# Quarter products with the weights' leading parts of both halves first, and three pieces moved in a two-layer encoder's feed-forward blocks

## The chip, the core and the metric

The kernel runs on one core of one Trainium2 chip. The metric is the device time of one execution in microseconds (us), lower is better. The core has four engines that matter here, each with a queue of its own that it works through in order: TensorE (PE in the profile, with PEld for its loads of the stationary operand), VectorE (DVE), ScalarE (ACT) and GpSimd (POOL). SP only issues DMA transfers.

## The reference

Two encoder layers over 512 tokens of width 1024. Each layer has a feed-forward block, an attention mixer, cross-attention to a memory, and a second feed-forward block. The change lies in the four feed-forward blocks, each of which computes

```
h = h + 0.5 * swiglu(rmsnorm(h, g), wg, wu, wd)

def swiglu(x, wg, wu, wd):
    return (jax.nn.silu(x @ wg) * (x @ wu)) @ wd        # 1024 -> 2816 -> 1024
```

in float32. In the order of the program they are called here the first to the fourth feed-forward block (layer 0 ffn1, ffn2, layer 1 ffn1, ffn2).

## The kernel before

A float32 operand is split in two parts: a leading part, rounded by ACT (`wh`, `sh`, `xh`, `t1h`, ...), and the rest, subtracted by DVE (`wl`, `sl`, `xl`, `t1l`, ...). A product of two split operands is three matmuls: leading by leading, leading weights by lower tokens, lower weights by leading tokens, the pairs (0, 0), (0, 1), (1, 0) in the code.

The 2816 hidden columns are 22 blocks of 128, taken in 11 pairs. Pair 0, the plain pair, is computed directly (`plain_pair`, into four banks of PSUM: a gate bank and an up bank for each of its two blocks). Its end, `plain_end`, turns the norm's factors into a tile R (four transposes and a DVE copy, L421), multiplies the two gate banks by R (the plain gate, L424) and calls `hidden`: Silu on ACT (L432) and two multiplications with the up banks on DVE (L434).

The ten other pairs use a scheme with seven products instead of eight over quarters: the 1024 rows are two halves of 4 tiles, the 512 tokens two halves of 256, and gate and up are the two column halves. A quarter of the weights is a 128x1024 tile (2 blocks z by 4 row tiles k); a token operand is one of x's quarters (`xs`) or one of the sums t1 to t4. `product` issues the matmuls of one quarter product: 2 z by 3 pairs of parts by 4 k, 24 matmuls of 128x256 into a bank whose left half holds z = 0 and whose right half z = 1. Per pair they are named by their token operand:

- `open_pair`: "11" into bank y, then a copy of y: for pair 1 into a corner of the result tile `gu` (L592), for later pairs into a second bank x (L595).
- `sum_pair`: "1" into bank z, "2" added onto y; then ACT copies y to `gu` (L619).
- `cross_pair`: "21" into x (for pair 1 a fresh bank, added to the copy by L630), "3" onto y; copies and sums follow (L644 on ACT, L645 on DVE).
- `close_pair`: "4" onto y (`lower`), "22" onto z (`upper`); it returns `gates`, which runs a pair later.

Before a product may add onto a bank, the copy or sum that reads the bank must be done. The leading part of a quarter that needs a sum (`s`, L611 and L661 on DVE) is made by ACT at L544, its lower part by DVE at L546. `wh` and `wl` have two buffers each, `sh` and `sl` one, so a new `wh` waits until PE has read an old one for the last time. The tile `gu` shares two buffers with the tiles `tq` that hold t1 to t4 before they are split.

The down products (h @ wd) come in three chunks. The first two are quarter products too (`paired_down`), the last (pairs 7 to 10) is direct: `down_products`, L844, 128x512 matmuls with weights `sh`, `sl` for the first output block. Some of that block's products are put around the last pair's closing, to keep PE supplied.

The code is written stage by stage. A scheduler then fixes the order of each engine's queue and the buffers; `high_priority()` lets what is in it go ahead of other work, and `behind(ins)` keeps what is in it after the instruction ins. So a line that moves in the code can move others in the queues.

Of the kernel before, what the change touches and what calls it, by code (L numbers as in the profile page):

```python
# [11 lines left out]
F32 = mybir.dt.float32  # L12
# [7 lines left out]
P = 128  # L20
S = 512
# [91 lines left out]
class Encoder:  # L113
# [205 lines left out]
    def ffn(self, pre):  # L319


        with ExitStack() as ctx:
            pool = lambda name: ctx.enter_context(self.tc.tile_pool(name=pre + name, bufs=1))
            f = self.f = SimpleNamespace(pre=pre, ctx=ctx, hp=pool("h"), tp=pool("t"), H={}, n=2, taken=None, own=False, low=None, gate=None, ahead=None, spread=None, macc=None,
                                        G=[])
            R = self.plain_pair()
            ends = [sum(CHUNKS[:c + 1]) // 2 for c in range(len(CHUNKS))]
            c = 0
            pair = self.open_pair(1)
            R()  # L330
            for p in range(1, FB // 2):
                final = p == FB // 2 - 1
                self.sum_pair(pair)
                hide = None
                if f.gate is not None:
                    f.gate, gate = None, f.gate
                    hide = gate(f.lowered)
                if p in ends and c not in PAIRED:
                    self.down(c)
                    c += 1  # L340
                self.cross_pair(pair)
                if hide is not None:
                    hide()
                if p == 2:
                    self.set_aside()
                if final:
                    early = self.block(c, 0, True)
                    f.ahead = self.leading
                    self.down_products(c, early, LEAD + REST, False, range(CHUNKS[c] - 4))
                    self.down_products(c, early, LEAD + REST, False, range(CHUNKS[c] - 4, CHUNKS[c] - 2))  # L350
                    self.close_pair(pair, True)
                    self.down(c, early)
                else:
                    old, pair = pair, self.open_pair(p + 1)
                    f.gate = self.close_pair(old, False)
                    if c in PAIRED and p == ends[c]:
                        if self.mem_r is None and c == 0:
                            self.mem_squares()
                        self.paired_down(c)
                        c += 1  # L360
                if self.mem_r is None:
                    self.mem_stats(p)
# [51 lines left out]
    def plain_end(self, banks, r):  # L414
        nc, f = self.nc, self.f
        p = self.bank("pb")
        f.R = f.tp.tile([P, S], F32, name="R", tag="R", bufs=1)
        with self.tc.high_priority():
            for i in range(QB):
                nc.tensor.transpose(p[:, i * P:(i + 1) * P], r[:, i:i + 1].to_broadcast([P, P]), self.ident)  # L420
            nc.vector.tensor_copy(f.R, p)  # L421
        gs = f.tp.tile([P, 1024], F32, name="gs", tag="gs")
        for b in range(2):
            f.gated = nc.vector.tensor_mul(gs[:, b * S:(b + 1) * S], banks[b][0], f.R)  # L424
        self.hidden(0, gs, [pp[1] for pp in banks])

    def hidden(self, p, gs, us):

# [132 lines left out]
    def product(self, bank, w, xs, first, late=False):  # L561

        half = len(xs)
        ops = [(z, a, b, k) for z in range(2) for a, b in ((0, 0), (0, 1), (1, 0)) for k in range(half)]
        if late:
            ops.sort(key=lambda op: op[3] == half - 1)
        for n, (z, a, b, k) in enumerate(ops):
            o = (z * half + k) * P
            self.nc.tensor.matmul(bank[:, z * 256:z * 256 + 256], w[a][:, o:o + P], xs[k][b],  # L569
                                  start=first and n == 0, stop=n == len(ops) - 1, skip_group_check=True)  # L570
# [8 lines left out]
    def open_pair(self, p):  # L579
        nc, f = self.nc, self.f  # L580
        pair = SimpleNamespace(p=p)
        pair.y = self.bank("pa")
        with self.tc.high_priority():
            pair.w11 = self.raw_quarter(p, 0)
            f.first = f.after
            if f.spread is not None and p == 1:
                f.after = self.loaded
            w = self.operand(pair.w11)
        self.product(pair.y, w, self.tokens("11"), True)
        pair.gu = f.tp.tile([P, 2048], F32, name="gu", tag="gu", bufs=2)  # L590
        if p == 1:
            nc.scalar.copy(self.corner(pair, 0, 0), self.halves(pair.y))  # L592
        else:
            pair.x = self.bank("pa")
            nc.scalar.copy(pair.x, pair.y)  # L595
        return pair

    def sum_pair(self, pair):

        nc, f, p = self.nc, self.f, pair.p  # L600
        pair.z = self.bank("pb")
        with self.tc.high_priority():
            pair.s = f.tp.tile([P, 1024], F32, name="s1", tag="s1", bufs=3)
            self.fetch(pair.s, p, 3, f.first)
            nc.gpsimd.dma_start(pair.s, self.quarter(p, 2), accum_op=OP.add)
            w = self.operand(pair.s, None, f.factored if p == 1 else None)
        with self.tc.high_priority():
            xs = self.tokens("1")
        self.product(pair.z, w, xs, True)
        with self.tc.high_priority():  # L610
            f.lowered = nc.vector.tensor_sub(pair.s, pair.s, pair.w11)  # L611
            if p == 2:
                f.low(f.lowered)
            xs = self.tokens("2")
            w = self.operand(pair.s)
            f.lowered = self.parted
        self.product(pair.y, w, xs, False)
        with self.tc.high_priority():
            nc.scalar.copy(self.corner(pair, 0, 1), self.halves(pair.y))  # L619

    def cross_pair(self, pair):
        nc, f, p = self.nc, self.f, pair.p
        with self.tc.high_priority(), self.behind(f.lowered if p == 1 else None):
            pair.w12 = self.raw_quarter(p, 1)
            w = self.operand(pair.w12)
        x = self.bank("pa") if p == 1 else pair.x
        self.product(x, w, self.tokens("21"), p == 1)
        c = self.corner(pair, 0, 0)
        if p == 1:
            nc.vector.tensor_add(c, c, self.halves(x))  # L630
        else:
            nc.scalar.copy(c, self.halves(x))
        with self.tc.high_priority():
            s = f.tp.tile([P, 1024], F32, name="s3", tag="s3", bufs=1)
            self.fetch(s, p, 2)
            with self.behind(f.led), self.behind(f.taken):
                nc.scalar.activation(s, s, AF.Copy, scale=-1.0)  # L637
            nc.gpsimd.dma_start(s, self.quarter(p, 0), accum_op=OP.add)  # L638
            w = self.operand(s)
            f.crossed = self.parted  # L640
        self.product(pair.y, w, self.tokens("3"), False)
        c = self.corner(pair, 1, 1)
        with self.tc.high_priority():
            f.taken = nc.scalar.copy(c, self.halves(pair.y))  # L644
        nc.vector.tensor_add(c, c, self.halves(pair.z))  # L645
# [1270 lines left out]
```

## Time and profile before

| | |
|---|---|
| median of 3 runs | 2026.74 us (2025.84, 2026.74, 2027.5) |
| the profiled execution | 2023.98 us, of which the profile's span is 2022.0 us |
| PE busy | 2004.7 us, 99% of the span |
| DVE, ACT, POOL busy | 1598.9, 1278.4, 350.0 us |
| mean granted TensorE clock | 0.999 |

In the rows below, the first number is the start in us from the beginning of the span, the second the time taken, then engine, line, operation, and the tiles out<-in; xN is a count of like instructions in a row, and brackets hold idle time of the engine before the row and what ended it. A PE row's time runs to the modelled end of its last matmul, so rows overlap; what a matmul costs PE is read from one row's start to the next one's.

### The profile page before, as it was taken

Reading aid. Unit: us, or ns where it says so; the run is one execution under the profiler, and the core shown is the slowest. Engines: PE = TensorE matmul, PEld = TensorE weight load, DVE = VectorE, ACT = ScalarE, POOL = GpSimd, SP = SyncE. Lnnn points to the kernel's source line nnn. Section 1 sums busy time; section 2 is a strip of 40 time slices with the busy share of each in tenths; the row PEclk is TensorE's granted clock in tenths of the full one; section 3 lists DMA queues with packets and bytes.
Section 4 is the critical chain, followed back from the end, with each engine's and each line's share of the span. In section 5 each row is a group of like instructions: output and inputs, shape, how many; then the busy total and the mean of one; then the engine's idle time right before and its main releaser. Section 6 shows DMA issues by size and latency. Waiting matters only on the chain.

```text
span 2022.0 us, 35264 instructions
## 1 busy us (share of the span) xinstructions
PE 2004.7 (99%) x13853; PEld 1840.3 (91%) x13853; DVE 1598.9 (79%) x2370; ACT 1278.4 (63%) x1955; POOL 350.0 (17%) x332
## 2 busy tenths in 40 slices
PE   9999999999999999999999999999999999999999
PEld 7999998888888889999989999988888888999997
DVE  8979776699676798888689798774668688979884
ACT  7766564557785566665557665645768566667572
POOL 1011001355521111000010101003453011010100
PEclk9999999999999999999999999999999999999999
DMA  7787755222331187776557877644224325777762
GB/s 234 195 218 191 197 166 160 91 89 84 103 122 64 62 237 186 207 199 170 155 176 208 209 195 198 178 139 138 84 79 136 94 74 153 205 205 197 193 183 91
DMA packets 102262, 316.52 MB, mean 157 GB/s; under 512 B 11472, under 2 KB 14672, under 8 KB 102096
## 3 DMA queue, kind: packets, MB, share of 16 engines
q1 hardware_dynamic: 85680, 257.12, 39.2%
q0 software_dynamic: 16128, 56.63, 16.2%
q8 instruction: 109, 1.79, 0.4%
q10 hardware_dynamic: 288, 0.52, 0.1%
q14 instruction: 57, 0.47, 0.1%
HBM read 301.64 MB, written 12.58 MB: 155 GB/s over the span
## 4 chain that ended last, share of the span: by engine, by line
PE 94%; DVE 3%; ACT 1%; issue 1%; DMA 0%; POOL 0%; SPq 0%; ACTq 0%; DVEq 0%; POOLq 0%
PE ps_pa L569 35%; PE ps_pb L569 14%; PE ps_pa L967 13%; PE ps_pa L913 5%; PE ps_pb L844 4%; PE ps_pa L844 4%; PE ps_pa L401 3%; PE ps_pb L1080 3%; PE ps_pa L1570 2%; PE ps_pa L1401 2%; PE ps_pb L913 2%; PE ps_pb L1133 2%; PE ps_pb L1106 1%; PE ps_pa L1300 1%; PE ps_pb L401 1%; DVE wl L546 1%
## 5 line engine op out<-in xcount | busy, mean ns | idle before, releaser
L169 ACT ACTIVATE wh<-wf 128x1024 fp32r<-128x1024 f32 (+1 forms) x155 | 154.5, 1003 | 175.8 <-issue 37.8
L544 ACT ACTIVATE wh<-s 128x1024 fp32r<-128x1024 f32 (+1 forms) x132 | 136.4, 1035 | 135.3 <-DVE s L611 43.9
L546 DVE TENSOR_TENSOR wl<-s,wh 128x1024 fp32r<-128x1024 f32 (+1 forms) x132 | 157.1, 1190 | 37.0 <-ACT wh L544 36.0
L544 ACT ACTIVATE wh<-wf 128x1024 fp32r<-128x1024 f32 (+1 forms) x132 | 134.7, 1020 | 75.5 <-PE ps_pa L569 48.0
L546 DVE TENSOR_TENSOR wl<-wf,wh 128x1024 fp32r<-128x1024 f32 (+1 forms) x132 | 154.4, 1172 | 27.2 <-ACT wh L544 27.2
L171 DVE TENSOR_TENSOR wl<-wf,wh 128x1024 fp32r<-128x1024 f32 (+1 forms) x110 | 128.7, 1175 | 41.9 <-ACT wh L169 40.1
L544 ACT ACTIVATE sh<-s 128x1024 fp32r<-128x1024 f32 (+1 forms) x92 | 94.1, 1023 | 66.9 <-PE ps_pa L569 24.6
L171 POOL TENSOR_TENSOR wl<-wf,wh 128x1024 fp32r<-128x1024 f32 (+1 forms) x45 | 99.9, 2221 | 204.9 <-ACT wh L169 142.9
L638 POOL DMA_DIRECT2D s<-l_ffn_wq x40 | 35.2, 879 | 542.9 <-ACT s L637 363.0
L546 DVE TENSOR_TENSOR sl<-s,sh 128x1024 fp32r<-128x1024 f32 (+1 forms) x92 | 108.1, 1176 | 22.7 <-ACT sh L544 22.4
L967 PE MATMUL ps_pa<-wh,xh 128*128 128x512 f32 x384 | 121.7, 398 | 0.0
L967 PE MATMUL ps_pa<-wh,xl 128*128 128x512 f32 x384 | 118.9, 391 | 0.0
L967 PE MATMUL ps_pa<-wl,xh 128*128 128x512 f32 x384 | 118.7, 390 | 0.0
L569 PE MATMUL ps_pa<-xh,wh 128*128 128x256 f32 x560 | 86.9, 276 | 0.0
L569 PE MATMUL ps_pa<-xl,wh 128*128 128x256 f32 x560 | 86.9, 276 | 0.0
L569 PE MATMUL ps_pa<-xh,wl 128*128 128x256 f32 x560 | 86.9, 276 | 0.0
L967 PEld LDWEIGHTS ps_pa<-wh,xl 128*128 128x128 f32 x384 | 72.1, 188 | 15.7
L967 PEld LDWEIGHTS ps_pa<-wl,xh 128*128 128x128 f32 x384 | 72.0, 188 | 15.5
L1095 ACT ACTIVATE e<-e,m 128x128 f32<-128x128 f32 (+3 forms) x128 | 70.7, 554 | 21.7 <-DVE m L1094 21.3
L967 PEld LDWEIGHTS ps_pa<-wh,xh 128*128 128x128 f32 x384 | 69.2, 188 | 12.3
L569 PEld LDWEIGHTS ps_pa<-xl,wh 128*128 128x128 f32 x560 | 74.2, 188 | 0.0
L569 PEld LDWEIGHTS ps_pa<-xh,wl 128*128 128x128 f32 x560 | 74.2, 188 | 0.0
(454 smaller groups left out, 6054.1 us busy)
## 6 DMA issues: line engine op xcount, KB each, us to landing
wf<-l_ffn_wq SPq DMA_DIRECT2D x120, 512.0 KB, 4.2
s<-l_ffn_wq SPq DMA_DIRECT2D x80, 512.0 KB, 4.6
s<-l_ffn_wq POOLq DMA_DIRECT2D x80, 512.0 KB, 7.4
wf<-l_w_in SPq DMA_DIRECT2D x48, 512.0 KB, 3.4
wf<-l_ffn_wd SPq DMA_DIRECT2D x32, 512.0 KB, 3.7
wf<-l_ffn_wdq SPq DMA_DIRECT2D x24, 512.0 KB, 4.3
wf<-l_ffn_wdq SPq DMA_DIRECT2D x24, 384.0 KB, 3.6
s<-l_ffn_wdq SPq DMA_DIRECT2D x16, 512.0 KB, 4.5
```

Source lines behind the costliest of these rows:

```text
L169: self.leading = nc.scalar.activation(wh[:, sl], w[:, sl], AF.Copy)
L171: eng.tensor_sub(wl[:, sl], w[:, sl], wh.bitcast(F32)[:, sl])
L401: nc.tensor.matmul(p, w[a][:, k * P:(k + 1) * P], xs[k][c], start=k == order[0] and a == c == 0, stop=k == order[-1] and a == 1)
L544: self.leading = nc.scalar.activation(h, t, AF.Copy)
L546: self.parted = nc.vector.tensor_sub(l, t, h.bitcast(F32))
L569: self.nc.tensor.matmul(bank[:, z * 256:z * 256 + 256], w[a][:, o:o + P], xs[k][b], start=first and n == 0, stop=n == len(ops) - 1, skip_g ...
L844: self.nc.tensor.matmul(bank, w[a][:, j * P:(j + 1) * P], h, start=j == a == e == 0 and c < len(CHUNKS) - 1, stop=j == nb - 1 and (a, e) = ...
L913: nc.tensor.matmul(banks[dd], w[g, k // 2][a][:, o:o + P], parts(k)[b], start=k == first and a == b == 0, stop=k == last and a == 1)
L967: nc.tensor.matmul(banks[j], xs[k][a][:, j * P:(j + 1) * P], w[b][:, kk * 512:kk * 512 + 512], start=k == a == b == 0, stop=k == KB - 1 an ...
L1080: nc.tensor.matmul(bank[:, o:o + n], a, b[:, :n], start=c == 0, stop=c == len(ops) - 1)
L1095: nc.scalar.activation(e, e, AF.Exp, bias=m[:, i:i + 1], scale=-1.0, accum_out=rs[:, i:i + 1])
L1133: nc.tensor.matmul(p[:, q0:q0 + n], vp[jb][:, h * P:(h + 1) * P], t[:, src:src + n], start=c == 0, stop=c == 7)
```

## The change

Four edits, all in the feed-forward blocks:

1. `product` runs the pairs of parts as the outer loop and z inside: leading weights for z = 0 and 1 with the leading tokens, the same with the lower tokens, then the lower weights for both. The matmuls are the same, in another order.
2. The copy of pair 1's y goes into a tile `sq` of its own instead of into `gu`, the sum at L630 (now L637) reads it there, and this copy and that of later pairs are given high priority.
3. The plain gate and `hidden` are no longer called ahead of `sum_pair` of pair 1 but after it, and behind the lower part of its second sum. The subtraction `f.low` for pair 0 moves behind that operand, too.
4. At a block's end the last pair's closing comes after four of the first down block's early products instead of after all six.

```diff
@@ ffn @@
                     self.down_products(c, early, LEAD + REST, False, range(CHUNKS[c] - 4))
+                    self.close_pair(pair, True)
                     self.down_products(c, early, LEAD + REST, False, range(CHUNKS[c] - 4, CHUNKS[c] - 2))
-                    self.close_pair(pair, True)
                     self.down(c, early)
@@ plain_end @@
-        for b in range(2):
-            f.gated = nc.vector.tensor_mul(gs[:, b * S:(b + 1) * S], banks[b][0], f.R)
-        self.hidden(0, gs, [pp[1] for pp in banks])
+
+        def gate(after):
+            with self.behind(after):
+                for b in range(2):
+                    f.gated = nc.vector.tensor_mul(gs[:, b * S:(b + 1) * S], banks[b][0], f.R)
+            self.hidden(0, gs, [pp[1] for pp in banks])
+
+        f.gate = gate
@@ product @@
-        ops = [(z, a, b, k) for z in range(2) for a, b in ((0, 0), (0, 1), (1, 0)) for k in range(half)]
+        ops = [(z, a, b, k) for a, b in ((0, 0), (0, 1), (1, 0)) for z in range(2) for k in range(half)]
@@ open_pair @@
-        if p == 1:
-            nc.scalar.copy(self.corner(pair, 0, 0), self.halves(pair.y))
-        else:
-            pair.x = self.bank("pa")
-            nc.scalar.copy(pair.x, pair.y)
+        with self.tc.high_priority():
+            if p == 1:
+                pair.x = self.xp.tile([P, S], F32, name="sq", tag="sq", bufs=2)
+                nc.scalar.copy(pair.x, pair.y)
+            else:
+                pair.x = self.bank("pa")
+                nc.scalar.copy(pair.x, pair.y)
@@ sum_pair @@
             f.lowered = nc.vector.tensor_sub(pair.s, pair.s, pair.w11)
-            if p == 2:
-                f.low(f.lowered)
             xs = self.tokens("2")
             w = self.operand(pair.s)
             f.lowered = self.parted
+            if p == 2:
+                f.low(f.lowered)
@@ cross_pair @@
         if p == 1:
-            nc.vector.tensor_add(c, c, self.halves(x))
+            nc.vector.tensor_add(c, self.halves(pair.x), self.halves(x))
```

ACT's queue at the start of the first feed-forward block, before (`s_402` is the sum tile s1 of pair 1, `s_503` its s3):

```order
L483 ACTIVATE t2h<-tq 128x1024
L483 ACTIVATE t4h<-tq 128x1024
L544 ACTIVATE sh<-wf 128x1024
L544 ACTIVATE wh<-s_402 128x1024
L544 ACTIVATE wh<-s_503 128x1024
L592 COPY gu<-ps_pa 128x2x256
L432 ACT_TABLE_LOAD
L432 ACTIVATE t<-gs 128x1024
L544 ACTIVATE wh<-wf 128x1024
L619 COPY gu<-ps_pa 128x2x256
```

and in the changed kernel, where s1 and s3 are `s_386` and `s_504`:

```order
L488 ACTIVATE t2h<-tq 128x1024
L549 ACTIVATE sh<-wf 128x1024
L488 ACTIVATE t4h<-tq 128x1024
L599 COPY sq<-ps_pa 128x512
L549 ACTIVATE wh<-s_386 128x1024
L549 ACTIVATE wh<-s_504 128x1024
L549 ACTIVATE wh<-wf 128x1024
L626 COPY gu<-ps_pa 128x2x256
L437 ACT_TABLE_LOAD
L437 ACTIVATE t<-gs 128x1024
```

The copy of y stands ahead of the leading parts of both sums instead of behind them, and the plain pair's Silu stands two instructions later.

DVE's queue at the same place, before:

```order
L611 TENSOR_TENSOR s_402<-s_402,wf 128x1024
L486 TENSOR_TENSOR t2l<-tq,t2h 128x1024
L424 TENSOR_TENSOR gs<-ps_pa,R 128x512 x2
L486 TENSOR_TENSOR t3l<-tq,t3h 128x1024
L546 TENSOR_TENSOR wl<-s_402,wh 128x1024
L546 TENSOR_TENSOR sl<-wf,sh 128x1024
L546 TENSOR_TENSOR wl<-s_503,wh 128x1024
L486 TENSOR_TENSOR t4l<-tq,t4h 128x1024
L434 TENSOR_TENSOR gs<-t,ps_pa 128x512
L434 TENSOR_TENSOR gs<-t,ps_pb 128x512
L661 TENSOR_TENSOR s_402<-wf,s_402 128x1024
L546 TENSOR_TENSOR wl<-wf,wh 128x1024
```

and in the changed kernel:

```order
L618 TENSOR_TENSOR s_386<-s_386,wf 128x1024
L491 TENSOR_TENSOR t2l<-tq,t2h 128x1024
L551 TENSOR_TENSOR wl<-s_386,wh 128x1024
L551 TENSOR_TENSOR sl<-wf,sh 128x1024
L427 TENSOR_TENSOR gs<-ps_pa,R 128x512 x2
L491 TENSOR_TENSOR t3l<-tq,t3h 128x1024
L551 TENSOR_TENSOR wl<-s_504,wh 128x1024
L491 TENSOR_TENSOR t4l<-tq,t4h 128x1024
L668 TENSOR_TENSOR s_386<-wf,s_386 128x1024
L551 TENSOR_TENSOR wl<-wf,wh 128x1024
L439 TENSOR_TENSOR gs<-t,ps_pa 128x512
L439 TENSOR_TENSOR gs<-t,ps_pb 128x512
```

The lower parts for "2" and "21" pass the plain gate, and the multiplications with the up banks stand two instructions later.

PE's queue at the end of the first feed-forward block, before (`hh`, `hl` are the hidden values, `xh` on `ps_pb` is product "22"):

```order
L844 MATMUL ps_pa<-hh,sh 128x512 x4
L844 MATMUL ps_pa<-hl,sh 128x512 x4
L844 MATMUL ps_pa<-hh,sl 128x512 x4
L844 MATMUL ps_pa<-hh,sh 128x512 x2
L844 MATMUL ps_pa<-hl,sh 128x512 x2
L844 MATMUL ps_pa<-hh,sl 128x512 x2
L569 MATMUL ps_pb<-xh,wh 128x256 x4
L569 MATMUL ps_pb<-xl,wh 128x256 x4
L569 MATMUL ps_pb<-xh,wl 128x256 x4
```

and in the changed kernel:

```order
L851 MATMUL ps_pa<-hh,sh 128x512 x4
L851 MATMUL ps_pa<-hl,sh 128x512 x4
L851 MATMUL ps_pa<-hh,sl 128x512 x4
L574 MATMUL ps_pb<-xh,wh 128x256 x8
L574 MATMUL ps_pb<-xl,wh 128x256 x8
L574 MATMUL ps_pb<-xh,wl 128x256 x8
L574 MATMUL ps_pa<-t4h,wh 128x256 x8
L574 MATMUL ps_pa<-t4l,wh 128x256 x8
L574 MATMUL ps_pa<-t4h,wl 128x256 x8
L851 MATMUL ps_pa<-hh,sh 128x512 x2
L851 MATMUL ps_pa<-hl,sh 128x512 x2
L851 MATMUL ps_pa<-hh,sl 128x512 x2
```

The two early down products stand behind 48 quarter matmuls instead of ahead of them, and each run of four within a product has become a run of eight.

## The prediction

> **What bounds the kernel now.** I read the page's first part, then the waits of PE, then the timeline around each of them.
>
> ```profile
> PE 2004.7 (99%) x13853; PEld 1840.3 (91%) x13853; DVE 1598.9 (79%) x2370; ACT 1278.4 (63%) x1955; POOL 350.0 (17%) x332
> ```
>
> PE works all the time, so a change that leaves the matmuls as they are can only gain what PE waits, or lose by new waits. The chain of waits shows the quarter products running undisturbed for long stretches:
>
> ```profile
> 58.63 13.60 PE ps_pa L569 x120
> ```
>
> That is 13.60 / 120 = 0.1133 us for each 128x256 matmul, 0.453 for a row of four, 2.72 for a product of 24, and twice 0.1133 for 128x512. All that PE waits in the span is in the waits of PE (total us, times, longest):
>
> ```profile
> PE ps_pa L569 <- ACT gu L592: 5.0, 3, 1.7
> PE ps_pa L569 <- DVE wl L546: 2.7, 3, 0.9
> PE ps_pa L844 <- DVE hl L457: 1.8, 4, 0.5
> PE ps_pb L228 <- DVE identb L127: 1.6, 1, 1.6
> PE ps_pa L569 <- ACT gu L644: 0.5, 1, 0.5
> ```
>
> Leaving out `identb`, which is the program's start, these are 10.0 us, all in the feed-forward blocks. The first two fall three times each: at the starts of the first, second and fourth block. The third falls once at each block's end. This is the first start, on PE:
>
> ```profile
> 33.47 0.73 PE L569 MATMUL ps_pb<-t1h,wh 128*128 128x256 f32 x4
> ...
> 35.86 0.62 PE L569 MATMUL ps_pb<-t1h,wl 128*128 128x256 f32 x4
> 38.13 0.73 PE L569 MATMUL ps_pa<-t2h,wh 128*128 128x256 f32 x4 [1.66 <-ACT gu L592]
> 38.70 0.62 PE L569 MATMUL ps_pa<-t2l,wh 128*128 128x256 f32 x4
> 40.23 0.72 PE L569 MATMUL ps_pa<-t2h,wl 128*128 128x256 f32 x4 [0.91 <-DVE wl L546]
> ...
> 42.15 0.62 PE L569 MATMUL ps_pa<-xh,sh 128*128 128x256 f32 x4
> ```
>
> A stall costs more than its idle time. From 38.70 to 40.23 are 1.53 us where 0.453 would do: 1.08 lost for 0.91 idle. The first row after a stall loses another 0.12 (38.13 to 38.70 is 0.57). So I count from row to row and not the idle time. From the start of "1" to that of "21" are 42.15 - 33.47 = 8.68 us, where 48 matmuls need 5.44.
>
> **The copy, the gate and the lower parts at a block's start.** ACT and DVE at this place:
>
> ```profile
> 35.60 2.01 ACT L544 ACTIVATE wh<-s 128x1024 fp32r<-128x1024 f32 x2 [1.63 <-DVE s L611]
> 37.52 0.56 ACT L592 COPY gu<-ps_pa 128x512 f32<-128x512 f32 x1
> ```
>
> ```profile
> 34.36 1.22 DVE L611 TENSOR_TENSOR s<-s,wf 128x1024 f32<-128x1024 f32 x1
> 35.49 1.22 DVE L486 TENSOR_TENSOR t2l<-tq,t2h 128x1024 fp32r<-128x1024 f32 x1
> 36.63 1.28 DVE L424 TENSOR_TENSOR gs<-ps_pa,R 128x512 f32<-128x512 f32 x2
> 37.83 1.22 DVE L486 TENSOR_TENSOR t3l<-tq,t3h 128x1024 fp32r<-128x1024 f32 x1
> 38.96 1.22 DVE L546 TENSOR_TENSOR wl<-s,wh 128x1024 fp32r<-128x1024 f32 x1
> 40.09 1.22 DVE L546 TENSOR_TENSOR sl<-wf,sh 128x1024 fp32r<-128x1024 f32 x1
> ...
> 43.50 0.68 DVE L434 TENSOR_TENSOR gs<-t,ps_pa 128x512 f32<-128x512 f32 x1
> ```
>
> y is complete before "1" starts at 33.47, but its copy stands behind both `wh`. In the changed queue it stands ahead of the first `wh`, where ACT sat idle for 1.63 us, longer than the copy's 0.56: the copy costs nothing. Its own tile also frees it from t2l's read of the buffer that `gu` shares. What is late next is the first `wh` itself: it waits for L611, which does not move, and ends near 36.65 (half of the 2.01). "2" can start at 36.70 instead of 38.13; undisturbed it would be 33.47 + 0.12 + 2.72 = 36.31.
>
> DVE steps are 1.13 us from start to start for 128x1024, 0.60 for the gate's two. In the new order t2l still runs from 35.49 to 36.71, then `wl` starts at 36.71, `sl` at 37.84, the gate at 38.97. "2" now needs `wl` after 16 matmuls (1.81 us) instead of 8 (0.91): at 38.5, and it is done at 37.93. The 0.91 is gone twice over, by edit 1 and by edit 3. If only one of them worked, edit 3 alone would still do: 36.82 + 0.91 = 37.73 against 37.93, a wait of 0.2.
>
> The gate's new place adds a wait. x of pair 1 takes the first plain gate's bank, which frees at 38.97 + 0.68 = 39.65; before, it was free at 37.3. "21" would be due at 36.70 + 0.12 + 2.72 = 39.54 and starts at 39.70, and loses 0.12 in its first row. Queued behind the gate are t3l, `wl` of "3" and t4l. The DVE work up to t4l is the same as before, so they come when they came (t3l 40.17, `wl` 41.30, t4l 42.44), while "3" starts at 39.82 + 2.72 = 42.54 and needs t3l 0.91 and `wl` 1.81 later. The plain Silu waits for the gate and for two more ACT instructions; the up multiplications (L434) go from 43.50 to 45.84, behind a sum and a lower part. They hold the up banks, which the changed program asks for only after "11" of pair 2: ahead of that product stands no wait for them.
>
> So "1" to "21" falls from 8.68 to 39.70 - 33.47 + 0.12 = 6.35 us: 2.33 gained. The other two starts, and the granted clock at the last (the third number from the end):
>
> ```profile
> 729.78 0.71 PE L569 MATMUL ps_pb<-t1h,wh 128*128 128x256 f32 x4
> ...
> 738.49 0.62 PE L569 MATMUL ps_pa<-xh,sh 128*128 128x256 f32 x4
> ...
> 1713.38 0.71 PE L569 MATMUL ps_pb<-t1h,wh 128*128 128x256 f32 x4
> ...
> 1723.44 0.85 PE L569 MATMUL ps_pa<-xh,sh 128*128 128x256 f32 x4
> ```
>
> ```profile
> 1720.00:1724.00 4.00, 3.85 (x19) 3.85 (x20) 4.00 (x5) 1.54 (x3) 0.00 (x0) 0.57 0.16 14
> ```
>
> 8.71 us in the second block: 2.36 gained. 10.06 in the fourth: 3.71 gained, of which 1.35 is that the clock fell to 0.57 right behind the two stalls; with stalls of 0.2 to 0.4 us I expect no such fall. The third block shows none of these waits and has nothing to gain here. Sum: 8.40.
>
> **Copies and order inside the block.** In the second block "4" waits for y's copy, which stands behind the hidden values of pair 0:
>
> ```profile
> 746.20 0.62 PE L569 MATMUL ps_pa<-xh,wl 128*128 128x256 f32 x4
> 747.29 0.74 PE L569 MATMUL ps_pa<-t4h,sh 128*128 128x256 f32 x4 [0.47 <-ACT gu L644]
> ```
>
> In the changed queue those hidden values stand behind the copy: 1.09 - 0.453 + 0.11 = 0.75 gained. In steady products edit 1 moves no matmul count and no weight load; `wh` frees 0.45 us earlier and `wl` is asked for 0.91 later. PE shows no waits there, so this gains nothing. POOL's queue keeps its order; SP's only exchanges neighbours (a weight quarter against copies of x, kept for later), which I cost at nothing, because each quarter is asked for a product or more after its transfer. If that cover were gone, a late quarter would cost its lateness plus 0.3 once a block.
>
> **The end of a block.** The two products moved behind the closing waited for `hl`:
>
> ```profile
> 289.27 0.63 PE L844 MATMUL ps_pa<-hh,sh 128*128 128x512 f32 x2
> 290.35 0.73 PE L844 MATMUL ps_pa<-hl,sh 128*128 128x512 f32 x2 [0.45 <-DVE hl L457]
> 290.91 0.62 PE L844 MATMUL ps_pa<-hh,sl 128*128 128x512 f32 x2
> 291.37 0.63 PE L569 MATMUL ps_pb<-xh,wh 128*128 128x256 f32 x4
> ```
>
> 2.10 us for 6 x 0.2267 = 1.36: 0.74 lost, four times, 2.96. In the new place two products (5.44 us) lie ahead of them, which covers the wait. What is asked for earlier is "22", by 2.1 us: it needs the sum of bank z ahead of it in DVE's queue. Its inputs (`wh` after 16 matmuls of "3", then the copy) come 0.45 earlier, so I take no wait; late by one DVE step it would cost 0.6 + 0.3, four times 3.6.
>
> **The sum** is 8.40 + 0.75 + 2.96 = 12.1 us of the profiled execution's 2023.98 (span 2022.0 and 1.98 around it): 2011.9. The median of the runs, 2026.74, is 2.76 above it, and the runs lie 1.66 apart. One fall of the clock costs 1.35, and there are three like places, of which the profiled execution was hit at one. If the timed runs were hit at up to three, up to 2 x 1.35 = 2.7 more goes. Nothing shown decides it; I take half, 1.3. Bounds of the rest: `wl` waits in front of weight loads that are not on PE's list could give up to 0.5 (an estimate, a third of a step at each block's start), and the moved gate could cost twice what I put (0.28 more, three times, 0.8). Forecast: 2026.74 - 12.1 - 1.3 = 2013.3, its own range 2010.5 (2.7 and 0.5 more) to 2017 (no clock gain beyond the profile's, and 2.4 lost).
>
> The Trainium skill, "TensorE: Matmul & The Clock Gate", section "Why this matters for your kernels", advises only against idle gaps above some 3 us. By that rule stalls of 1.69 and 0.90 us would not set the clock back, the fall at 1720 would have another cause and stay, and the sum would be 1.35 smaller. The trace here speaks against it, since the fall follows the stalls directly; but two like stalls had none.
>
> **The rivals.**
>
> *The wait moves to the delayed gate (12 in 100).* DVE has no slack in these first 15 us, so 2.3 us later up multiplications and the sums behind them may hold PE after all. By the steps above the sum of z before "22" of pair 1 ends at 50.6, and PE would come for it at 39.82 + 4 x 2.72 = 50.7: no slack. A further wait of one 1.13 us step with 0.3 around it, at three starts, takes back 4.3: 2013.3 + 4.3 = 2017.6. Against it: the queue's steps add up to no wait.
>
> *The clock's fall is not of the stalls (7 in 100).* Then only 12.1 - 1.35 = 10.7 is gained: 2016.0.
>
> *The change doesn't do what it says (6 in 100).* DVE, saturated there, sets the start, and PE gets only the ends of the blocks, 2.96: 2023.8.
>
> *Slower: each change of bank half costs (4 in 100).* In a product the half of the bank is now changed five times instead of once. There are 98 products a block (70 in ten pairs, 28 in two paired down chunks), so 4 x 98 x 4 = 1568 more changes. From 12.1 / 1568 = 8 ns each on, nothing is gained; at 11 ns the kernel is 4 us slower than before, at 20 ns it takes 2026.74 - 12.1 + 31.4 = 2046. Against it: the 0.1133 us per matmul includes a change every 12 matmuls and a new bank every 24, and no row shows a step there.
>
> **How the numbers follow.** The forecast has 71 in 100. A measurement of this kernel can tell about 0.2%, 4.05 us. Forecast, moved wait and clock are faster by more: 0.90. The third rival is within it: 0.06. The last is slower: 0.04. The range 2010.5 to 2019 takes in the forecast and the first two rivals with one more such wait, and leaves out the other 10 in 100.
>
> **What would show it.** In the profile after: no wait of PE for the copy of y, for `wl` or for `hl`; at the three starts "1" to "21" near 6.3 us with one short wait for the first `wh` or the copy ahead of "2" and one for the gate (now L427); "22" at the end straight behind four products; a span near 2010; the granted clock at 1.00 throughout. A PE wait for L439, L652 or `sl` around 45 to 52 us would show the first rival, a product slower than 2.72 us the last. The prediction is wrong if the quarter products' own pace changes, or if PE, early by 2 us, meets a transfer that was just in time.

## The result, and the profile after

The changed kernel takes 2017.58 us (median of 4 runs, 2012.75 to 2018.23) beside 2027.12 for the kernel before: a ratio of 0.9946, 95% interval 0.9928 to 0.9964. So it is faster, by 9.5 us, where 13.4 were forecast. Its profiled execution has a span of 2016.1 us (2022.0 before) and took 2018.23, where the sum said 2011.9.

What PE waits in the quarter products, in the waits of PE (total us, times, longest; the rows left out belong to the program's start and to the attention):

```profile
...
PE ps_pa L574 <- ACT wh L549: 1.3, 4, 0.5
...
PE ps_pa L574 <- ACT gu L626: 0.4, 1, 0.4
...
```

The waits for the copy (5.0), for `wl` (2.7), for `hl` (1.8) and for the second block's copy (0.5) are gone; in the blocks 1.3 for `wh` and 0.4 for a copy are new: 10.0 us of idle time in the blocks became 1.7. Yet PE is busier than before, with the same matmuls (2004.7 us before):

```profile
PE 2006.9 (100%) x13853; PEld 1845.5 (92%) x13853; DVE 1592.6 (79%) x2370; ACT 1279.9 (63%) x1955; POOL 350.3 (17%) x332
```

The first block's start, on PE:

```profile
33.51 1.17 PE L574 MATMUL ps_pb<-t1h,wh 128*128 128x256 f32 x8
...
36.75 1.21 PE L574 MATMUL ps_pa<-t2h,wh 128*128 128x256 f32 x8 [0.26 <-ACT wh L549]
37.80 1.10 PE L574 MATMUL ps_pa<-t2l,wh 128*128 128x256 f32 x8
...
39.75 1.21 PE L574 MATMUL ps_pa<-xh,sh 128*128 128x256 f32 x8
40.80 1.11 PE L574 MATMUL ps_pa<-xl,sh 128*128 128x256 f32 x8
41.74 1.10 PE L574 MATMUL ps_pa<-xh,sl 128*128 128x256 f32 x8
...
51.16 1.10 PE L574 MATMUL ps_pb<-xh,wh 128*128 128x256 f32 x8
```

"1" to "21" is 39.75 - 33.51 = 6.24 us (8.68 before, 6.35 forecast). But look at the rows of eight: 40.80 to 41.74 is 0.94 us, 0.1178 a matmul, where 8 x 0.1133 = 0.907 was usual before. A product now takes 2.83 us instead of 2.72. The chain of waits shows how long this lasts:

```profile
56.98 14.13 PE ps_pa L574 x120
76.77 14.13 PE ps_pa L574 x120
125.36 13.60 PE ps_pa L574 x120
...
751.95 14.13 PE ps_pa L574 x120
...
1058.06 13.60 PE ps_pa L574 x120
```

14.13 / 120 = 0.1178 from the start to the first paired down products near 95 us, again near 752 and, not shown, near 1733; 13.60 afterwards and in the whole third block. I call the two the slow and the fast pace. The granted clock is not the reason, as the row of the four us in which it fell before shows (1.00, third number from the end):

```profile
1720.00:1724.00 4.00, 4.00 (x36) 4.00 (x36) 4.00 (x6) 2.51 (x4) 0.00 (x0) 1.00 0.82 293
```

The closing of the first block on PE, with "22" behind four of the early products and the two moved ones behind "4":

```profile
287.80 1.08 PE L851 MATMUL ps_pa<-hh,sl 128*128 128x512 f32 x4
288.71 1.08 PE L574 MATMUL ps_pb<-xh,wh 128*128 128x256 f32 x8
...
294.17 0.62 PE L851 MATMUL ps_pa<-hh,sh 128*128 128x512 f32 x2
294.63 0.62 PE L851 MATMUL ps_pa<-hl,sh 128*128 128x512 f32 x2
295.09 0.62 PE L851 MATMUL ps_pa<-hh,sl 128*128 128x512 f32 x2
295.55 1.52 PE L851 MATMUL ps_pb<-hh,wh 128*128 128x512 f32 x6
```

294.17 to 295.55 is 1.38 us for 6 matmuls of 0.2267 (1.36), where it was 2.10: no wait for `hl`. "22" follows its four products without a wait, too.

An account of all four blocks, from the starts of successive matmuls, as us above 0.1133 and 0.2267 each:

| excess over the steady pace, us | before | after | difference |
|---|---|---|---|
| stalls and the matmuls next to them | 12.43 | 4.55 | -7.88 |
| fall of the clock behind a stall | 1.50 | 0.00 | -1.50 |
| the down products at the closings | 2.85 | -0.16 | -3.01 |
| matmuls 115 to 124 ns apart (the slow pace) | 0.71 (155) | 7.25 (1617) | +6.54 |
| sum | 17.49 | 11.64 | -5.85 |

The sum agrees with the spans (-5.9). The stalls that the forecast named are gone; 6.5 us of the gain were given back by a slower pace that no term held.

### The profile page after: what moved, and what is told of

It is laid out like the page before. It is cut to its first block, busy times and chain, and to the rows that moved or that the text cites. A ratio compares the mean times of both kernels' runs of the same rounds, so it can differ in the third digit from the quotient of the medians.

```text
span 2016.1 us, 35267 instructions
## 1 busy us (share of the span) xinstructions
PE 2006.9 (100%) x13853; PEld 1845.5 (92%) x13853; DVE 1592.6 (79%) x2370; ACT 1279.9 (63%) x1955; POOL 350.3 (17%) x332
## 4 chain that ended last, share of the span: by engine, by line
PE 95%; DVE 2%; ACT 2%; DMA 1%; issue 1%; POOL 0%; SPq 0%; ACTq 0%; POOLq 0%; DVEq 0%
PE ps_pa L574 35%; PE ps_pb L574 14%; PE ps_pa L974 13%; PE ps_pa L920 5%; PE ps_pa L851 4%; PE ps_pb L851 4%; PE ps_pa L401 3%; PE ps_pb L1087 3%; PE ps_pa L1577 2%; PE ps_pa L1408 2%; PE ps_pb L920 2%; PE ps_pb L1140 2%; PE ps_pb L1113 1%; PE ps_pa L1307 1%; PE ps_pb L401 1%
## 5 line engine op out<-in xcount | busy, mean ns | idle before, releaser
L645 POOL DMA_DIRECT2D s<-l_ffn_wq x40 | 35.2, 880 | 526.1 <-ACT s L644 341.4
L574 PE MATMUL ps_pa<-xh,wh 128*128 128x256 f32 x560 | 75.6, 277 | 0.0
L574 PE MATMUL ps_pa<-xh,wl 128*128 128x256 f32 x560 | 75.6, 277 | 0.0
L574 PE MATMUL ps_pa<-xl,wh 128*128 128x256 f32 x560 | 75.6, 277 | 0.0
L612 POOL DMA_DIRECT2D s<-l_ffn_wq x40 | 36.8, 919 | 210.3 <-DVE tq L481 73.0
L574 PEld LDWEIGHTS ps_pa<-xh,wh 128*128 128x128 f32 x560 | 69.2, 188 | 0.0
```

## The experiments

Each kernel ran beside runs of the kernel before on its chip (medians 2026.51, 2026.65 and 2027.20 in the three groups). A slow stretch in the last column is one of over 100 successive matmuls, counted in the one profiled execution of each. The ratios are close to those of the means, not of the medians.

| kernel | median us (range; runs) | ratio to before [95%] | slow stretches (matmuls) |
|---|---|---|---|
| changed kernel | 2017.58 (2012.75 to 2018.23; 4) | 0.9946 [0.9928, 0.9964] | 3 (491, 491, 491) |
| e1 order alone | 2021.75 (2018.81 to 2026.58; 11) | 0.9976 [0.9967, 0.9985] | 3 (478, 664, 477) |
| e2 all but the order | 2015.94 (2014.19 to 2016.91; 5) | 0.9948 [0.9934, 0.9961] | 0 |
| e3 return, same tokens | 2015.01 (2013.04 to 2016.40; 5) | 0.9944 [0.9932, 0.9957] | 0 |
| e4 snake, no return | 2017.72 (2015.38 to 2018.46; 5) | 0.9955 [0.9943, 0.9968] | 2 (490, 374) |
| e5 return, other tokens | 2016.18 (2014.82 to 2017.88; 5) | 0.9948 [0.9936, 0.9961] | 0 |
| e6 closing alone | 2023.58 (2020.83 to 2028.35; 11) | 0.9983 [0.9974, 0.9992] | 0 |
| e7 alternate, no return | 2016.34 (2013.72 to 2021.39; 5) | 0.9952 [0.9938, 0.9966] | 1 (492) |
| e8 return in "21" of pair 1 | 2014.17 (2012.36 to 2014.84; 5) | 0.9937 [0.9924, 0.9949] | 0 |
| e9 copies and gate alone | 2019.78 (2017.78 to 2023.22; 8) | 0.9969 [0.9960, 0.9979] | 0 |
| e10 other order in "21", no return | 2018.51 (2015.22 to 2021.63; 6) | 0.9964 [0.9950, 0.9977] | 4 (490, 616, 373, 618) |
| e11 changed kernel again | 2016.97 (2015.36 to 2023.81; 6) | 0.9961 [0.9947, 0.9976] | 2 (373, 373) |
| e12 e8 again | 2016.29 (2011.16 to 2022.56; 7) | 0.9954 [0.9937, 0.9971] | 2 (373, 374) |

The theory: what keeps PE slow is the new order of the products, because in it no product goes back from the lower part of the weights to the leading one. The rival: short stalls set the slow pace, whatever the order.

**e1, the order alone**, on the kernel before:

```diff
-        ops = [(z, a, b, k) for z in range(2) for a, b in ((0, 0), (0, 1), (1, 0)) for k in range(half)]
+        ops = [(z, a, b, k) for a, b in ((0, 0), (0, 1), (1, 0)) for z in range(2) for k in range(half)]
```

> The kernel before with the product order alone changed (leading parts of both halves first). The copies, the gate and the closing stay as before. Theory A (in the new order a stretch at 117.9 ns per matmul, once begun, doesn't end by itself): the three waits for wl go (2.7 us idle, about 3.6 with what a stall adds), the waits of 1.7 us for the copy stay, and behind them the quarter products run at 117.9 ns until the first paired down product, about 7.5 us in three blocks: 2027.1 - 3.6 + 7.5 = 2031, slower than before. Theory B (only a short stall sets the slow pace, a long one resets it, and the order is innocent): 2027.1 - 3.6 = 2023.5, or 2022.2 if the fall of the clock goes too. The profile decides between them by the rows of 8 behind the 1.7 us wait: 0.943 us apart by A, 0.907 by B.

The median lies below both numbers; the profiled execution, the slowest of the eleven (2026.58), shows the reason, in its chain:

```profile
60.63 14.13 PE ps_pa L569 x120
...
760.25 13.60 PE ps_pa L569 x120
...
1741.50 14.13 PE ps_pa L569 x120
```

The 1.68 us wait for the copy stands ahead of all three, and the pace behind it is slow, fast, slow. So a long stall doesn't reset the pace, which ends theory B; nor does the order always lead into the slow one, as A had it. The order permits it, and something that differs from place to place chooses. A stretch of 664 also began at 129.5 us, behind a wait of 0.32. The waits for `wl` on PE's list are gone, as both said. The order alone still gains 4.8 us at the median, where A had it slower than before; part of that is the clock, of which more below.

**e2, all but the order** (the same two lines exchanged, on the changed kernel):

> The changed kernel with the product order of before (one half of the bank after the other); copies, gate and closing stay changed. Theory A: in the old order a slow stretch ends in the second half of the same product, so the 7.5 us come back; wl is asked for 0.9 us earlier, a wait of about 0.2 + 0.3 at three starts, 1.5 at most: 2017.6 - 7.5 + 1.5 = 2011.6 (2010 to 2013). Theory B: the short stalls stay, so does the slow pace: 2017.6 to 2019. Rows of 4 behind '2' are 0.453 apart by A and 0.471 by B.

The profile follows A: short stalls stand at the starts where the changed kernel's do, and no slow stretch lasts longer than a product. The time is 4 us above A's number, and these are stalls: 8.97 us by the account, where the changed kernel has 4.55, since ACT's queue is ordered anew with the products and `wh` comes late at five places:

```profile
PE ps_pa L574 <- ACT wh L549: 2.4, 5, 0.8
```

A wait for `wl` is left as well, though PE's list has none. It stands in front of the weight load (PEld), in "2" of the first block:

```profile
37.68 0.53 PEld L574 LDWEIGHTS ps_pa<-t2h,wl 128*128 128x128 f32 x4 [0.27 <-DVE wl L551]
```

The two intervals between matmul starts there are 348 and 224 ns, together 0.35 us more than two steady ones, and much the same at the other two starts.

**e3 and e4, two more orders**, each a list of rows (half of the bank, part of the weights, part of the tokens) on the changed kernel:

```diff
+        ops = [(z, a, b, k) for z, a, b in ((0, 0, 0), (0, 0, 1), (1, 0, 1), (0, 1, 0), (1, 0, 0), (1, 1, 0)) for k in range(half)]   # e3
+        ops = [(z, a, b, k) for z, a, b in ((0, 0, 0), (1, 0, 0), (1, 0, 1), (0, 0, 1), (0, 1, 0), (1, 1, 0)) for k in range(half)]   # e4
```

> The changed kernel with a third order: wh on the first half (hh, lh), lh of the second half, wl of the first half, then back to wh for hh of the second half, wl of the second half. The lower part is asked for after 12 matmuls (8 in the old order, 16 in the changed one), and as in the old order the weights go back from the lower to the leading part inside the product, with the same tokens. If that return is what ends a slow stretch (theory A1): no lasting slow pace, and no wait for wl: 2010.5 to 2012. If it is the number of changes between the halves of the bank (theory A2, 3 to 5 changes here, 1 in the old order): the slow pace stays, 2017 to 2018.

> The changed kernel with the rows of each product in a snake: hh first half, hh second, lh second, lh first, hl first, hl second. The leading parts still come first and the lower ones last, with no return, but the half of the bank changes 3 times instead of 5. Theory A1 (the missing return from the lower to the leading part keeps the slow pace): as the changed kernel, 2017 to 2018. Theory A2 (each change of half costs while the pace is slow): the loss of 7.5 us shrinks to 3/5 or less, 2014.6 or below. By the prediction's slower rival, which prices every change of half alike, the products in the fast blocks would also fall below 2.72 us.

e3 has no slow stretch, with three changes of half; e4, also with three, has two, so the changes of half (A2) are not it. The first product of a block is the sharpest test, since "11" of pair 1, straight behind the 512-wide plain products, begins at the slow pace in all 14 profiles and all four blocks. On PE of the kernel before:

```profile
30.32 0.63 PE L569 MATMUL ps_pa<-xh,sh 128*128 128x256 f32 x4
30.80 0.63 PE L569 MATMUL ps_pa<-xl,sh 128*128 128x256 f32 x4
31.27 0.63 PE L569 MATMUL ps_pa<-xh,sl 128*128 128x256 f32 x4
31.73 0.63 PE L569 MATMUL ps_pa<-xh,sh 128*128 128x256 f32 x4
32.20 0.62 PE L569 MATMUL ps_pa<-xl,sh 128*128 128x256 f32 x4
32.66 0.62 PE L569 MATMUL ps_pa<-xh,sl 128*128 128x256 f32 x4
33.12 0.60 PE L420 MATMUL ps_pb<-ident,factor 128*128 128x128 f32 x4
```

In e3:

```profile
30.42 0.63 PE L574 MATMUL ps_pa<-xh,sh 128*128 128x256 f32 x4
30.89 1.11 PE L574 MATMUL ps_pa<-xl,sh 128*128 128x256 f32 x8
31.83 0.63 PE L574 MATMUL ps_pa<-xh,sl 128*128 128x256 f32 x4
32.30 0.63 PE L574 MATMUL ps_pa<-xh,sh 128*128 128x256 f32 x4
32.77 0.62 PE L574 MATMUL ps_pa<-xh,sl 128*128 128x256 f32 x4
33.23 0.60 PE L420 MATMUL ps_pb<-ident,factor 128*128 128x128 f32 x4
```

In the changed kernel:

```profile
30.32 1.10 PE L574 MATMUL ps_pa<-xh,sh 128*128 128x256 f32 x8
31.26 1.11 PE L574 MATMUL ps_pa<-xl,sh 128*128 128x256 f32 x8
32.21 1.10 PE L574 MATMUL ps_pa<-xh,sl 128*128 128x256 f32 x8
33.15 0.60 PE L420 MATMUL ps_pb<-ident,factor 128*128 128x128 f32 x4
```

Before, rows of four stand 0.47 us apart up to 32.20, then 0.46. Between the single starts the last slow interval is the 15th; the return from `sl` to `sh` stands after the 12th matmul. In e3, where the return comes after the 16th, it is the 19th. In the changed kernel all 24 are slow. It is the same in each of the 56 cases: the five kernels with the return after 12 (before, e2, e5, e6, e9) are free from the 16th on in 20 of 20, e3 from the 20th on in 4 of 4, and the eight kernels without a return in that product never in it, 32 of 32. Moving the return moved the release. In every order with a return that was tried, the return also goes over to the other half of the bank. The change of half alone releases nothing (the eight kernels without a return have it, too); a return within one half was not tried.

**e5, the return with other tokens** (hh, lh, hl of the first half, then lh of the second):

```diff
+        ops = [(z, a, b, k) for z, a, b in ((0, 0, 0), (0, 0, 1), (0, 1, 0), (1, 0, 1), (1, 0, 0), (1, 1, 0)) for k in range(half)]
```

> The changed kernel with the order hh, lh, hl of the first half up to the lower part, then lh of the second half (back to wh, but with the other tokens xl, not with the xh that the lower part has just used), hh and hl of the second half. Theory A1, return of the weights alone: no lasting slow pace, as in the old order, 2014.5 to 2016.5 (the stall ahead of '2' and the ACT order as with the old order). Rival (the return counts only with the same tokens on both sides of it, as in the old order): stretches at 117.9 ns of hundreds of matmuls, 2017.5 to 2020.

No slow stretch, and the fast pace three matmuls behind the return: what the tokens are doesn't matter.

**e7, the half of the bank changed at every matmul:**

```diff
+        ops = [(z, a, b, k) for a, b in ((0, 0), (0, 1), (1, 0)) for k in range(half) for z in range(2)]
```

> The changed kernel with the half of the bank changed at every matmul (23 changes in a product instead of 5), leading parts first. It prices the change of half by itself, the prediction's slower rival: 18 more changes x 392 products = 7056; at 4.5 ns each 32 us slower than the changed kernel (2049), at nothing no slower. Theory A1 says that a change costs nothing (113.3 ns in the fast blocks with 5 changes as with 1), so 2011 to 2018, with lasting slow stretches, since no weight goes back from the lower to the leading part.

2016.34 beside the changed kernel's 2017.58, where 2049 was the price at 4.5 ns a change: a change of half costs nothing that shows. In the third block, where neither has a slow stretch, e7 and the changed kernel's second profile (e11) take 260.39 us each from "11" to the end of the last pair's closing, with 18 more changes in each product of e7. The prediction's slower rival is refuted by this.

**e8, the return in one product alone,** and **e10, its control,** both on the changed kernel:

```diff
-        ops = [(z, a, b, k) for a, b in ((0, 0), (0, 1), (1, 0)) for z in range(2) for k in range(half)]
+        ops = [(z, a, b, k) for z, a, b in (((0, 0, 0), (0, 0, 1), (1, 0, 1), (0, 1, 0), (1, 0, 0), (1, 1, 0)) if back else ((0, 0, 0), (1, 0, 0), (0, 0, 1), (1, 0, 1), (0, 1, 0), (1, 1, 0))) for k in range(half)]
...
-        self.product(x, w, self.tokens("21"), p == 1)
+        self.product(x, w, self.tokens("21"), p == 1, back=p == 1)
```

In e10 the first list is (0, 0, 0), (0, 0, 1), (1, 0, 0), (1, 0, 1), (0, 1, 0), (1, 1, 0): rows of four, no return.

> The changed kernel with only the product '21' of pair 1 in the order of the run before (wh on the first half, lh of the second half, wl of the first, back to wh, wl of the second): 24 matmuls of a block take another order, every other engine's queue is the same to the row, and so are the stalls ahead of '2' and '21'. Theory A1 (the return to the leading part ends the slow stretch, and nothing else begins one): the products behind '21' run at 113.3 ns, about 516 slow matmuls a block fewer, 3 x 516 x 0.0045 = 7.0 us: span near 2009.5, time 2011 to 2012. Rival (the changed order slips into the slow pace by itself within a few products, whatever happened at the start): 2017 to 2018, rows of 8 at 0.943 us again from '3' on or soon behind.

> The control of that: the same product '21' of pair 1 in another order again, but without a return: hh and lh of the first half, hh and lh of the second, then hl of both. Its rows are of four like those with the return, and all else is as in the changed kernel. If the return is what ends the slow pace: as the changed kernel, slow stretches of some 520 matmuls in some blocks, 2015 to 2018.5. If rows of four or any other order in that product do it: no slow stretches, 2012.5 to 2015.

e8 came out with no slow stretch, a span of 2010.5 and the profiled execution at 2012.36, close to the sum of the prediction (2011.9). The median, 2014.17, is 2 us above what was expected. "21" in its first block, slow up to the return and fast behind it:

```profile
40.73 1.10 PE L574 MATMUL ps_pa<-xl,sh 128*128 128x256 f32 x8
41.67 0.63 PE L574 MATMUL ps_pa<-xh,sl 128*128 128x256 f32 x4
42.14 0.63 PE L574 MATMUL ps_pa<-xh,sh 128*128 128x256 f32 x4
42.61 0.62 PE L574 MATMUL ps_pa<-xh,sl 128*128 128x256 f32 x4
43.06 1.07 PE L574 MATMUL ps_pa<-t3h,wh 128*128 128x256 f32 x8
```

The same place in e10, in which no other queue differs either, slow to the end and beyond:

```profile
40.78 0.63 PE L574 MATMUL ps_pa<-xl,sh 128*128 128x256 f32 x4
41.25 0.63 PE L574 MATMUL ps_pa<-xh,sh 128*128 128x256 f32 x4
41.72 0.64 PE L574 MATMUL ps_pa<-xl,sh 128*128 128x256 f32 x4
42.20 1.10 PE L574 MATMUL ps_pa<-xh,sl 128*128 128x256 f32 x8
43.14 1.10 PE L574 MATMUL ps_pa<-t3h,wh 128*128 128x256 f32 x8
```

This one block of e8 is the test. In its second and fourth block "21" was at the fast pace within seven matmuls, ahead of the return, behind the hitch that the product begins with; that these blocks stayed fast was chance. And three of e10's four stretches begin later than "21". In all profiles "21" of pair 1 came to a return at the slow pace three times (here, and in the second and fourth block of e3) and was fast from the 20th interval on each time; without a return it was slow there eight times and stayed so to its end.

**e11 and e12, the changed kernel and e8 once more,** on e10's chip:

> The changed kernel as it is, once more, beside the two kernels that differ from it in one product. Theory A1 with chance (each interruption leaves PE in the fast or the slow pace by chance, and the changed order can't leave the slow one): times spread by up to three times 2.3 us, 2011 to 2018.5, and the profile has slow stretches of some 520 matmuls in some of the blocks 1, 2 and 4, not the same number in every profile, and in none where no short stall stands behind the start. If the slow pace is fixed by the program: the same three stretches as in the first profile, and times within 2 us.

> The changed kernel with the return to the leading part in '21' of pair 1 alone, for the comparison with the changed kernel on one chip: no slow stretch of over 100 matmuls in any block, 2012.5 to 2015, 2 to 4 us below the changed kernel.

The slow stretches are not fixed by the program: e11 has two, where the first profile of the same kernel had three. And e12 contradicts what was expected of it, and a part of e8's theory. Its "21" was fast within five matmuls of its start in all three blocks, ahead of the return, but "22" of pair 1 starts with a hitch too short for the list of waits, and behind it, in the second and fourth block, the slow pace began again:

```profile
745.12 1.07 PE L574 MATMUL ps_pa<-t4h,sl 128*128 128x256 f32 x8
746.02 1.14 PE L574 MATMUL ps_pb<-xh,wh 128*128 128x256 f32 x8
747.00 1.10 PE L574 MATMUL ps_pb<-xl,wh 128*128 128x256 f32 x8
747.94 1.10 PE L574 MATMUL ps_pb<-xh,wl 128*128 128x256 f32 x8
```

The first row is 0.90 long, the second 0.98 (0.07 more), all that follow 0.94. So an interruption, even a short one, can be a new draw, and one product with a return is no cure; every product needs it, as in e2, e3 and e5. e8's first 3 us of advantage over the changed kernel were in part luck: on one chip, 2016.29 and 2016.97 can't be told apart.

**e6 and e9, the terms by themselves.** e6 is the kernel before with only the closing moved, e9 the changed kernel with the old order and the old closing:

```diff
-                    self.down_products(c, early, LEAD + REST, False, range(CHUNKS[c] - 4, CHUNKS[c] - 2))
                     self.close_pair(pair, True)
+                    self.down_products(c, early, LEAD + REST, False, range(CHUNKS[c] - 4, CHUNKS[c] - 2))
```

> The kernel before with only the closing of the last pair moved ahead of the two down products. By the prediction's term: the four waits for hl go and '22' meets no new one, 2.96 us: 2026.5 - 3.0 = 2023.5. If '22' waits for the sum of z instead: no gain, or up to 3.6 less that, about 2027.

> The copies and the gate alone: the product order and the closing of before, the rest as changed. By the prediction's terms: the block starts give 8.4 (of which 1.35 the clock, which fell in one start of the profiles so far), y's copy 0.75, less a wait of 0.2 + 0.3 for wl at three starts: 2026.6 - 7.1 - 0.8 + 1.5 = 2020.2 (2018.5 to 2021.5). If the gain of the starts hangs on the product order instead: above 2023.

e6 gains 3.07 us (2023.58), e9 7.4 (2019.78): both as expected. Together 10.5, and e2, which has both, gained 10.6. These edits make a gain as large as that of the whole change; the new order on top of them moved the median from 2015.94 to 2017.58 and 2016.97, that is, it cost 1 to 1.6 us (not clear of the noise).

No version is shown to beat the changed kernel: the intervals overlap. I would take e3, whose median is the lowest of the kernels with a return in every product.

## Why the prediction was right, and where it was wrong

- **Starts.** Forecast 8.40 with the clock. The three starts went from 8.68, 8.71 and 10.06 us to between 6.24 and 6.25. DVE's and ACT's steps came within 0.1 us of the forecast ones: `wl` at 36.73, the gate at 39.01, L439 at 45.89, L652 from 49.95 to 50.63. The copy, the gate and the lower part cost what was said. Without the new order (e9) the wait for the copy is gone, too, and of that for `wl` what the text had said is left, 0.2: it shows in the weight loads, 0.27 as in e2. "1" to "21" takes 6.45 us there, so of the gain at a start edit 1 made 0.2 us.
- **Closings.** Forecast 2.96; 3.01 in the account, 3.07 as the difference of medians in e6.
- **The first rival** (a further wait of a whole DVE step behind the delayed gate) didn't come. "22" came 0.5 us later than forecast, because of the slow pace, so this trace alone doesn't price it; with the fast pace the hitch at "22" was 0.07 (e12).
- **The step that failed** is in the second part: "In steady products edit 1 moves no matmul count and no weight load; ... so this gains nothing." Gain it did not, but it cost 6.5 us of the profiled execution. The pace was taken to be a constant of 0.1133 us, though the kernel before already showed the other one at 30.32 us, in rows of 0.47 that end within the product; what ends them was not asked. The slower rival had the right place (the new order of a product) and the wrong mechanism: it priced the change of half, which is free (and its 4 us at 11 ns should be 5 by the 12.1 that it starts from), and its sign of recognition, "a product slower than 2.72 us", is what the profile showed. The prediction had also named what would make it wrong, "if the quarter products' own pace changes", and that came, though the time stayed within the range.
- **The clock.** 1.35 in the sum and 1.3 beside it rested on one fall at 1720 us. The pair of stalls (1.7 us for the copy, 0.9 for `wl`) stands at six places in the profiles of the kernel before and e6, and the clock fell behind one of them; behind the 1.68 us alone, at three places in e1, it never did. What the timed runs lost can be read from the mean granted clock on record for each of them. The share that wasn't granted, times the span, is 3.5 us on average in the 45 runs of the kernel before beside the experiments and 3.3 in e6, which keeps the stalls, but 1.7 in e1, 1.5 in e9 and 1.2 in the ten runs of the changed kernel. The runs of the kernel before at 0.999 took 2025.2 us on average, at 0.998 2027.0, at 0.997 2029.3. So some 2.3 us of clock were gained, where 1.35 and 1.3 had been put: the guess of a half was nearly right. (A single run's clock, given to 0.001, is coarse, 2 us; the averages carry this. Where in those runs the clock fell is inferred from which edits kept it up, and not shown.) Some falls are not of the block starts, and the change doesn't touch them. Five us at the program's start in e12, and then in the changed kernel's first profile (granted clock third from the end):

```profile
8.00:13.00 5.00, 4.55 (x12) 0.66 0.96 374
```

```profile
8.00:13.00 5.00, 4.87 (x20) 1.00 0.93 354
```

The kernel before had 1.00 there too. A mean of 0.66 over 5 us is 3.4 us at half rate, 1.7 us lost. Six of the 14 profiles have it (e1, e6, e7, e9, e11, e12), and their first "11" stands at 32.0 to 32.5 us instead of 30.0 to 31.0. The Trainium skill, "TensorE: Matmul & The Clock Gate", section "What's actually happening", gives a free-running window of about 3.4 us after which the rate is set anew; the length agrees. That it is an idle window of that length which sets it back does not: from PE's first matmul to these falls no wait is longer than 1.5 us.

The median came 4.3 us above the forecast. Some 0.4 of it is clock that was not gained. The rest is about two slow stretches of 2.2 us (491 x 0.0045), and the changed kernel's two profiles have three and two; how many the timed runs had is not on record. 2017.58 lies above the forecast's own range (up to 2017; its lower end is 2011.4 by its terms, not 2010.5) and within the one given with the rivals (up to 2019), whose upper part had been meant for a moved wait. That the slower pace stayed within it was luck.

## What to carry to other kernels

One stream of matmuls can run at two paces, here 4% apart, for hundreds of matmuls, at a granted clock of 1.00 and without a wait; so compare start-to-start times of steady rows, not only waits, when an order is changed. Where a stretch of slow rows ends by itself in the kernel at hand, find out what ends it before the order that does so is given up. And a sum built on one profile needs the events that come by chance (here the clock and the pace) counted over several. Where PE's list shows no wait, look at the waits of its weight loads, too.

## What the runs showed of the hardware that was not expected

- In these streams of 128x128 weight loads and 128x256 matmuls PE has two paces, 113.3 and 117.8 ns. In both, a load starts 2 to 4 ns after the preceding matmul; the matmul follows its load by 110 ns in the fast and 114 to 116 in the slow one (single starts in the changed kernel's trace).
- Which of them follows an interruption is decided within a few matmuls and differs from execution to execution of one program. Behind the wait for `wh` at the first block's start the intervals were 222, 117, 118, 118 ns and slow from there on in the changed kernel's first profile, 223, 114, 124, 118, 113 and fast in e8, with the same wait (0.26 and 0.27).
- A return of the weights to the leading part within a product ends the slow pace three matmuls later, in 24 of 24 cases with "11"; without one the pace stays slow for all of that product, in 32 of 32. Why it does is open. So is why the return from one product's lower part to the next product's leading part doesn't: there the bank, the tokens and the tile of weights change too, which was not taken apart.
- The Trainium skill, "TensorE: Matmul & The Clock Gate", section "Back-to-back issue gap", says that the spacing of such pairs is set by both the load and the matmul. By its formula there for an isolated matmul and the one in "LDWEIGHTS (loading the stationary operand)" the two would take about 109 and 107 ns here (estimates), so nearly the same; 113.3 and 117.8 were measured from matmul to matmul. Whether this has to do with the two paces no run here shows.
